# Decoder step on one core: attention by groups of 512 queries, the output projection between the groups, and part of a multiply on GpSimd

## The chip, the core and the metric

The kernel runs on one core of a Trainium2 chip. A core has five engines with in-order queues of their own: TensorE (PE in the profile; PEld are its weight loads), VectorE (DVE), ScalarE (ACT), GpSimd (POOL) and SyncE (SP), which here only issues DMAs. Engines wait for each other by semaphores. SBUF is the memory that all of them use, PSUM the one that TensorE writes; PSUM has eight banks of 128 x 512 float32. The metric is the device time of one execution, in microseconds, lower is better.

## What is computed

One step of a small decoder trunk: a state-space layer, a K/V projection and one layer of stick-breaking attention, for a prompt of 2048 tokens and eight single-token samples. The change lies in the attention layer of the prompt and the output projection behind it:

```python
def sb_attend(q, k, v, bias, q_pos, k_pos):       # 16 heads of 64
    z = einsum('bqhd,bkhd->bhqk', q, k) * HEAD_DIM ** -0.5 + bias
    mask = k_pos[None, :] < q_pos[:, None]        # strictly causal
    log_1m = where(mask, log_sigmoid(-z), 0.0)
    log_stick = cumsum(log_1m, axis=3, reverse=True) - log_1m
    w = where(mask, exp(log_sigmoid(z) + log_stick), 0.0)
    return einsum('bhqk,bkhd->bqhd', w, v)
...
x = x + gate * rms_norm((o * silu(z)) @ w_out_b, g_post_b)   # the projection, 1024 x 1024
```

The kernel forms s = sigmoid(z), c = 1 - s, a running product of c from the right (the stick that is left), and w = s times that product.

## The kernel before, in words

The last phase, `phase_b2`, holds the attention and the output projection. Its work is cut into 320 units. A unit is one head `h` of a head pair `hp`, one block `m` of 256 queries (or its upper or lower 128, `par`), and the lower or upper 1024 keys (`half`), of which `n` columns are not masked. Wide units (`par` is 0 or 1) have n = 640, 768, 896 or 1024; in narrow ones (`par` is None) both 128-row parts lie in one tile, with n = 256 or 512 each. The order of the units was: all of one head pair, block by block m = 0 to 7, upper keys before lower ones.

For each unit `front` does the following. TensorE forms the scores in PSUM tiles psZ (two float32r matmuls for each 512 columns, since the query is held as a high and a low part). ScalarE writes s = sigmoid of them. GpSimd writes c = 1 - s into a tile `cc` (L1417, and L1399 for narrow units); a memset puts 1.0 behind the last column (L1419, L1398). VectorE scans `cc` from the right with a product (L1426, L1402; its second operand `zero` lies in PSUM), and multiplies s by the scanned `cc` (L1427, L1403). Where a row of keys goes on in the other half, a copy of one column carries the product over (L1423).

```python
rev = cc[:, 0:n][:, ::-1]
nc.vector.tensor_tensor_scan(rev, rev, zero.to_broadcast([128, n]), init, OP.mult, OP.add)
nc.vector.tensor_mul(s[:, :n], s[:, :n], cc[:, 1:n + 1])
```

Three units later (`LAG`), `back` transposes the weights on TensorE (L54) and ScalarE copies them out of PSUM (L1443). Once both heads of a pair are there, `vals` multiplies them with the values. At the lower keys VectorE multiplies by the gate `zb` (L1469), the result is split in a high and a low part (L1470, L1471) and stored to `yT` in DRAM. Between units TensorE also works on the eight samples (`sample_vals`, pages of 2048 cached keys each) and the output weights are loaded and split (`stage_w`, L864 and L865).

Only when the attention is done come the 16 tiles of 128 rows of the output projection and one of 8 sample rows: `out_rows` loads a tile of `yT` and of the residual `x`, `out_proj` does 48 matmuls of 128 x 512, a norm (L906 to L912) and the sum with the residual, half on GpSimd and half on VectorE (L913).

Within one engine the instructions stand in the order that the scheduler of the framework gave them when the program was built; it is not the order of the Python text in every place. Each engine then works through its list in order.

Of the kernel before, what the change touches and what calls it, by code (L numbers as in the profile page):

```python
# [8 lines left out]
FT = mybir.dt.float32  # L9
# [8 lines left out]
D = 1024  # L18
SEQ = 2048
# [16 lines left out]
LAG = 3  # L36

# [5 lines left out]
class Kern:  # L43
# [29 lines left out]
    def run(self):  # L73
        with ExitStack() as ctx:
            tc = self.tc
            self.turn = 1
# [52 lines left out]
    def psZ(self):  # L129
        return self.ps.tile([128, 512], FT, tag="Z", name="psZ", bufs=3)  # L130
# [761 lines left out]
    def out_proj(self, xpool, M, yhi, ylo, cols, whi, wlo, x, G, dst, two=False):  # L892
# [3 lines left out]
        self.turn ^= 1  # L896
        if not two:
            p = self.psB()
            p = [p[:, 0], p[:, 1]]
        else:  # L900
            p = [self.psZ(), self.psZ()] if self.turn else [self.psA(), self.psA()]
        self.tm_r(p, M, yhi, ylo, cols, whi, wlo)
        ss = xpool.tile([128, 2], FT, tag="ss", name="ss")[:M]
        for h in range(2):
            jk = (self.rp.tile([128, 512], BF, tag="wraw", name="jk") if two else xpool.tile([128, 512], BF, tag="jk", name="jk"))[:M]
            nc.scalar.activation(jk, p[h][:M], AF.Square, accum_out=ss[:, h:h + 1])  # L906
        nc.vector.tensor_add(ss[:, 0:1], ss[:, 0:1], ss[:, 1:2])
        rs = self.rsqrt(xpool, ss[:, 0:1], M, 1, "rs")
        for h in range(2):
            c = slice(h * 512, h * 512 + 512)  # L910
            xo = self.rp.tile([128, 512], FT, tag="wraw", name="xo")[:M] if two else xpool.tile([128, 512], FT, tag="xo", name="xo")[:M]
# [149 lines left out]
    def phase_b1(self):  # L1061
# [7 lines left out]
        with ExitStack() as c:  # L1069
# [96 lines left out]
            for s, (ps, t) in enumerate(steps):  # L1166
# [14 lines left out]
                if s == 15:  # L1181
                    self.load_x(0, 0)
                    self.load_q(0, 0)
# [154 lines left out]
    def rot(self, kind, shape, dt=FR):  # L1338

        first, n = {"X": (0, 6), "V": (6, 3), "Q": (9, 2), "s": (11, 4), "y": (15, 1), "o": (0, 9)}[kind]  # L1340
# [4 lines left out]
    def load_x(self, hp, half):  # L1345

        nc = self.nc
        for h in (2 * hp, 2 * hp + 1):
            t = self.rot("X", [128, 1024])
            nc.sync.dma_start(t.bitcast(FT), dram(self.kT, h * 128 * SEQ + half * 1024, [[SEQ, 128], [1, 1024]]))  # L1350
            self.X[h, half] = t
        t = self.rot("V", [128, 8, 128], FT)
        nc.sync.dma_start(t, dram(self.O["p_v"], half * 1024 * D + hp * 128, [[D, 128], [128 * D, 8], [1, 128]]))
# [10 lines left out]

    def phase_b2(self):
        nc, tc, I, O = self.nc, self.tc, self.I, self.O
        self.yT = self.scr("yT", [2, D, NC1])
        with ExitStack() as c:
# [4 lines left out]
            samples = self.sample_vals(sp)  # L1373
            wload = self.stage_w("w1", I["w_out_b"], D, 0)
            X, V, Q = self.X, self.V, self.Q

            def front(u):
# [5 lines left out]
                cc = ap.tile([128, 1028], FT, tag="cc", name="cc", bufs=LAG + 2)  # L1383
                bias = self.sbias[:, h:h + 1]
                if par is None:
                    for a in range(2):
                        q = slice(a * 128, a * 128 + 128)
                        L = n if a else n - 128
                        z = self.psZ()
# [191 lines left out]
```

## Time and profile before

| | us |
|---|---|
| median of 3 runs (3326.25 to 3329.0) | 3328.98 |
| the profiled execution | 3336.95 |
| its span, first to last instruction | 3335.2 |
| last phase in it: attention, 1986.6 to 3139.1 | 1152.5 |
| last phase in it: the rest of the projection, 3139.1 to the end | 196.1 |

The profiled execution is 8 us slower than the median of the runs and 1.75 us longer than its own span. The last phase begins at 1986.6 us with the memset of `zero` (L1476); the last multiply of the attention on VectorE ends at 3139.1 us. A busy time is the time in which an engine had an instruction in it; for TensorE the ends of matmuls are modelled, so that the distance between starts says more.

### The profile page before, as it was taken

Reading aid. Unit: us, or ns where it says so; the run is one execution under the profiler, and the core shown is the slowest. Engines: PE = TensorE matmul, PEld = TensorE weight load, DVE = VectorE, ACT = ScalarE, POOL = GpSimd, SP = SyncE. Lnnn points to the kernel's source line nnn. Section 1 sums busy time; section 2 is a strip of 40 time slices with the busy share of each in tenths; the row PEclk is TensorE's granted clock in tenths of the full one; section 3 lists DMA queues with packets and bytes.
Section 4 is the critical chain, followed back from the end, with each engine's and each line's share of the span. In section 5 each row is a group of like instructions: output and inputs, shape, how many; then the busy total and the mean of one; then the engine's idle time right before and its main releaser. Section 6 shows DMA issues by size and latency. Waiting matters only on the chain.

```text
span 3335.2 us, 56710 instructions
## 1 busy us (share of the span) xinstructions
PE 2980.9 (89%) x19352; PEld 2349.6 (70%) x19352; DVE 2402.6 (72%) x4220; ACT 1310.6 (39%) x2954; POOL 682.5 (20%) x856
## 2 busy tenths in 40 slices
PE   7899899999999899988699998888888888888898
PEld 4667667778888898987588875555555555555677
DVE  7699997354445456666656539999999999899734
ACT  4422221332224433334232326556555655655311
POOL 1234343000000000001010103333223322333211
PEclk7999999999999899999899999999999999999999
DMA  7433333664543566667666674545345454534353
GB/s 216 133 95 106 99 95 93 193 186 122 157 140 110 173 188 191 192 201 218 189 198 197 200 209 135 157 126 166 116 135 156 137 151 123 160 113 121 89 170 127
DMA packets 488099, 506.91 MB, mean 152 GB/s; under 512 B 57605, under 2 KB 377382, under 8 KB 487618
## 3 DMA queue, kind: packets, MB, share of 16 engines
q1 hardware_dynamic: 482962, 501.88, 51.3%
q8 instruction: 154, 2.52, 0.3%
q10 hardware_dynamic: 4560, 1.35, 0.2%
q14 instruction: 135, 1.11, 0.1%
q0 software_dynamic: 288, 0.06, 0.0%
HBM read 372.39 MB, written 130.75 MB: 151 GB/s over the span
## 4 chain that ended last, share of the span: by engine, by line
PE 34%; DVE 32%; DMA 12%; issue 9%; ACT 4%; SPq 3%; POOL 2%; DVEq 0%; ACTq 0%; POOLq 0%
PE psA L49 20%; DVE cc L1426 9%; PE psB L49 5%; PE psZ L49 5%; DMA kp<-in_cache_k 5%; DVE s L1427 4%; PE psC L54 3%; DVE cc L1402 2%; DVE kp L1249 2%; PE psC L49 1%; DVE s L1403 1%; DVE zs L1250 1%; DVE A L563 1%; ACT s L1416 1%; POOL cc L1417 1%
## 5 line engine op out<-in xcount | busy, mean ns | idle before, releaser
L1426 DVE TENSOR_TENSOR_SCAN cc<-cc,zero 128x1024 f32<-128x1024 f32 (+3 forms) x256 | 538.0, 2108 | 49.4 <-POOL cc L1417 41.4
L54 PE MATMUL psC<-idf,s 128*128 128x128 f32 x2176 | 319.8, 287 | 146.3 <-ACT wT L1443 72.3
L1417 POOL TENSOR_SCALAR cc<-s 128x1024 f32<-128x1024 f32 (+3 forms) x256 | 291.0, 1139 | 643.4 <-ACT s L1416 401.3
L54 PEld LDWEIGHTS psC<-idf,s 128*128 128x128 f32 x2176 | 249.6, 146 | 211.5 <-ACT wT L1443 111.7
L49 PE MATMUL psZ<-X,Q 128*128 128x512 f32 (+2 forms) x1280 | 370.8, 409 | 20.3 <-ACT s L1416 15.5
L1416 ACT ACTIVATE s<-psZ,sbias 128x512 f32<-128x512 f32 (+2 forms) x512 | 310.1, 663 | 197.0 <-PE psZ L49 180.5
L1443 ACT ACTIVATE wT<-psC 128x512 f32<-128x512 f32 (+3 forms) x640 | 314.0, 549 | 64.4 <-PE psC L54 63.4
L1427 DVE TENSOR_TENSOR s<-s,cc 128x1024 f32<-128x1024 f32 (+3 forms) x256 | 305.3, 1201 | 13.6 <-DVE cc L1426 0.5
L1249 DVE TENSOR_TENSOR kp<-kp,qb 128x512 f32<-128x512 f32 x256 | 180.2, 708 | 186.3 <-DMA kp<-in_cache_k 159.9
L49 PE MATMUL psA<-hi,w0h 128*128 128x256 f32 (+1 forms) x1024 | 304.4, 297 | 10.6 <-DVE z L1103 3.8
L49 PEld LDWEIGHTS psZ<-X,Q 128*128 128x128 f32 x1280 | 220.6, 198 | 119.2 <-issue 74.2
L49 PE MATMUL psA<-hi,w0l 128*128 128x256 f32 (+1 forms) x1024 | 294.8, 288 | 2.6 <-DVE w0l L865 2.6
L49 PE MATMUL psA<-lo,w0h 128*128 128x256 f32 (+1 forms) x1024 | 294.8, 288 | 0.2 <-DVE lo L843 0.2
L49 PE MATMUL psA<-wT,V 128*64 128x256 f32 (+1 forms) x2304 | 285.1, 384 | 9.7 <-DVE cc L1423 5.8
L49 PEld LDWEIGHTS psA<-wT,V 128*64 128x64 f32 x2304 | 166.8, 141 | 109.2 <-issue 27.0
L1051 POOL TENSOR_TENSOR lo<-h,hi 128x256 fp32r<-128x256 f32 x92 | 75.8, 833 | 787.7 <-ACT hi L1050 642.1
L49 PEld LDWEIGHTS psA<-hi,w0h 128*128 128x128 f32 x1024 | 201.4, 197 | 13.0 <-DVE z L1103 4.6
L49 PEld LDWEIGHTS psA<-hi,w0l 128*128 128x128 f32 x1024 | 200.4, 196 | 3.3 <-DVE w0l L865 3.3
L49 PEld LDWEIGHTS psA<-lo,w0h 128*128 128x128 f32 x1024 | 201.2, 196 | 0.8 <-POOL lo L1051 0.5
L1250 DVE TENSOR_REDUCE zs<-kp 128x8 f32<-128x512 f32 x256 | 173.9, 683 | 5.6
L913 POOL TENSOR_TENSOR x<-x,xo 128x512 f32<-128x512 f32 x32 | 42.0, 1314 | 590.0 <-DVE xo L912 590.0
L49 PE MATMUL psA<-ghi,w0h 128*128 128x256 f32 (+1 forms) x512 | 149.6, 292 | 1.4 <-ACT sg L966 1.4
(412 smaller groups left out, 6784.0 us busy)
## 6 DMA issues: line engine op xcount, KB each, us to landing
kp<-in_cache_k SPq DMA_DIRECT2D x256, 256.0 KB
vp<-in_cache_v SPq DMA_DIRECT2D x256, 256.0 KB
Q<-qT SPq DMA_DIRECT2D x128, 256.0 KB
x<-x SPq DMA_DIRECT2D x50, 512.0 KB
x<-in_x_prompt SPq DMA_DIRECT2D x32, 512.0 KB
qT<-kq SPq DMA_DIRECT2D x128, 128.0 KB
kT<-kq SPq DMA_DIRECT2D x128, 128.0 KB
X<-kT SPq DMA_DIRECT2D x32, 512.0 KB
```

The lines of the kernel that those rows point to most:

```text
L49: self.nc.tensor.matmul(out, lhsT, rhs, start=start, stop=stop, skip_group_check=True)
L54: self.nc.tensor.transpose(out, in_, self.idf[b:b + n, b:b + n])
L913: (nc.vector if h else nc.gpsimd).tensor_add(x[:, c], x[:, c], xo)
L1051: (nc.gpsimd if k % 2 or kept else nc.vector).tensor_sub(lo[:, k, :256], h, hi[:, k, :256].bitcast(FT))
L1249: nc.vector.tensor_mul(kp, kp, qb)
L1250: nc.vector.tensor_reduce(zs[:, pg, a * 8:a * 8 + 8], kp.rearrange("p (h d) -> p h d", h=8), axis=mybir.AxisListType.X, op=OP.add)
L1402: nc.vector.tensor_tensor_scan(rev, rev, zero.to_broadcast([128, n]), 1.0, OP.mult, OP.add)
L1416: nc.scalar.activation(s[:, b:b + w], z, AF.Sigmoid, scale=0.125, bias=bias)
L1417: nc.gpsimd.tensor_scalar(cc[:, :n], s[:, :n], -1.0, 1.0, OP.mult, OP.add)
L1426: nc.vector.tensor_tensor_scan(rev, rev, zero.to_broadcast([128, n]), init, OP.mult, OP.add)
L1427: nc.vector.tensor_mul(s[:, :n], s[:, :n], cc[:, 1:n + 1])
L1443: nc.scalar.activation(wT[h][:, b:b + nb, a * 128:a * 128 + 128], p[:, :nb * 128].rearrange("p (b q) -> p b q", b=nb), AF.Copy)
```

## The change

Blocks of 256 queries are taken in pairs, in five groups: (3, 2), (7, 6), (5, 4), (1), (0). A group runs over all head pairs before the next begins, so that its 512 (or 256) rows of `yT` are complete when it ends. From the third group on, steps of the output projection of finished groups (`out_tiles`, 15 steps for a tile) are put between the units; the two tiles of the last group come at the end. The samples and the output weights are done in the first two groups (192 units). Keys, values, queries and gates are loaded by a look-ahead (`loads`), since they are now needed again in each group.

`front` is split in `score` and `weigh`: the text calls `weigh` of a unit behind `score` of the next one. The scan covers n + 1 columns, its start value comes from a small tile `car`. In `weigh` VectorE multiplies only the first `own` columns and GpSimd the rest: 640 and 384 of 1024, 640 and 256 of 896, 512 and 256 of 768, 512 and 128 of 640, 384 and 128 in each part of a narrow unit of 512. `cc` has 3 buffers instead of 5, psZ 2 instead of 3; the two value blocks of a group share one PSUM bank (`psO`). In the projection both halves of the sum with the residual are on GpSimd.

```diff
+GROUPS = ((3, 2), (7, 6), (5, 4), (1,), (0,))
+OUT_STEPS = 15
...
-            def front(u):
+            def score(u):
...
-                cc = ap.tile([128, 1028], FT, tag="cc", name="cc", bufs=LAG + 2)
+                cc = ap.tile([128, 1028], FT, tag="cc", name="cc", bufs=3)
...
+                nc.gpsimd.memset(cc[:, n:n + 1], 1.0)
                 nc.gpsimd.tensor_scalar(cc[:, :n], s[:, :n], -1.0, 1.0, OP.mult, OP.add)
-                if diag:
-                    nc.gpsimd.memset(cc[:, n:n + 1], 1.0)
-                    init = 1.0
-                else:
-                    prev = carry[h, par]
-                    nc.vector.tensor_copy(cc[:, n:n + 1], prev)
-                    init = prev
-                rev = cc[:, 0:n][:, ::-1]
-                nc.vector.tensor_tensor_scan(rev, rev, zero.to_broadcast([128, n]), init, OP.mult, OP.add)
-                nc.vector.tensor_mul(s[:, :n], s[:, :n], cc[:, 1:n + 1])
-                carry[h, par] = cc[:, 0:1]
-                return s
+                return s, cc
...
+            def weigh(u, s, cc):
+
+                hp, m, half, h, par, n = u
+                own = n - n // 128 * 3 // 8 * 128
...
+                first = half or m < 4
+                rev = cc[:, 0:n + 1][:, ::-1]
+                nc.vector.tensor_tensor_scan(rev, rev, zero.to_broadcast([128, n + 1]),
+                                             1.0 if first else carry.pop((h, m, par)), OP.mult, OP.add)
+                if half:
+                    carry[h, m, par] = ap.tile([128, 1], FT, tag="car", name="car", bufs=12)
+                    nc.vector.tensor_copy(carry[h, m, par], cc[:, 0:1])
+                nc.vector.tensor_mul(s[:, :own], s[:, :own], cc[:, 1:own + 1])
+                if own < n:
+                    nc.gpsimd.tensor_mul(s[:, own:n], s[:, own:n], cc[:, own + 1:n + 1])
...
             for i, u in enumerate(us):
...
+                s, cc = score(u)
+                pend.append((u, s))
+                loads(i + 1)
+                if scored:
+                    weigh(*scored)
+                scored = u, s, cc
...
+                if gi < 2:
+                    if i * 64 // (sw - 8) < (i + 1) * 64 // (sw - 8):
+                        next(samples, None)
+                    if i % 8 == 5:
+                        next(wload, None)
...
+                else:
+                    if i == starts[gi] + 8:
+                        t = [2 * mm + a for mm in GROUPS[gi - 1] for a in range(2)]
+                        tiles.extend(t)
+                        steps += OUT_STEPS * len(t)
+                    cols = n * (2 if par is None else 1)
+                    k = -(-steps * cols // left)
+                    left -= cols
+                    for _ in range(min(k, steps)):
+                        next(outs, None)
+                        steps -= 1
                 if len(pend) > LAG:
                     back(*pend.pop(0))
...
-            for i in range(1, 16):
-                if i < 15:
-                    ins.append(self.out_rows(xp, i + 1))
-                if i == 8:
-                    self.out_samples(rows, xp)
-                self.out_tile(rows, xp, i, *ins.pop(0))
+            tiles.extend(2 * GROUPS[-1][0] + a for a in range(2))
+            tiles.append(None)
+            flush(outs)
...
+    def out_tiles(self, rows, xp, tiles):
...
+            y = [xp.tile([128, KT, M], FR, tag=f"o{a}{M}", name=f"o{a}{M}") for a in range(2)]
+            for a in range(2):
+                self.nc.sync.dma_start(y[a].bitcast(FT), dram(self.yT, a * D * NC1 + t * 128, [[NC1, 128], [128 * NC1, KT], [1, M]]))
...
+            yield
+            if late:
+                next(late)
+            yield
+            if late:
+                next(late, None)
+            yield
+            p = [self.psA(), self.psA()]
...
+                    if i % 4 == 0 and i < 48:
+                        yield
+            late = self.out_end(rows, t, M, p, x, G)
+            yield
...
+            nc.vector.scalar_tensor_tensor(xo, p[h][:M], rs, G[:M, c], OP.mult, OP.mult)
+            nc.gpsimd.tensor_add(x[:, c], x[:, c], xo)
```

The first place is GpSimd's list in the middle of the attention. In the program before it held, for each unit, the operation c = 1 - s (`cc` from `s`) and a memset, and nothing that needs the scan of that unit:

```order
L1417 TENSOR_SCALAR cc_28533<-s_28532 128x1024
L1417 TENSOR_SCALAR cc_28559<-s_28558 128x1024
L1419 MEMSET cc_28598 128x1
L1417 TENSOR_SCALAR cc_28598<-s_28597 128x640
L1419 MEMSET cc_28625 128x1
L1417 TENSOR_SCALAR cc_28625<-s_28624 128x768
```

So GpSimd could make the next unit's c while VectorE was still scanning. The same engine in the second group of the changed program, with five successive units (their s is 28748, 28773, 28868, 28897 and 28929), where L1462 is the new multiply of a unit's last 384 columns and needs that unit's scan:

```order
L1462 TENSOR_TENSOR s_28748<-s_28748,cc_28749 128x384
L1429 MEMSET cc_28898 128x1
L1462 TENSOR_TENSOR s_28773<-s_28773,cc_28774 128x384
L1429 MEMSET cc_28930 128x1
L1430 TENSOR_SCALAR cc_28869<-s_28868 128x1024
L1430 TENSOR_SCALAR cc_28898<-s_28897 128x1024
L1462 TENSOR_TENSOR s_28868<-s_28868,cc_28869 128x384
L1429 MEMSET cc_29028 128x1
L1430 TENSOR_SCALAR cc_28930<-s_28929 128x1024
L1462 TENSOR_TENSOR s_28897<-s_28897,cc_28898 128x384
```

The multiply of unit 28773 now stands ahead of the c of the unit after it, 28868; for unit 28868 it is the other way round, since the c of 28897 is made first. Counted over the whole list, the c of the next unit stands behind the multiply of a unit in 151 of 288 places and ahead of it in 137. The list of VectorE for the same units:

```order
L1455 SCALAR_TENSOR_TENSOR cc_28774<-cc_28774,car_28461,zero_24053 128x1025
L1460 TENSOR_TENSOR s_28773<-s_28773,cc_28774 128x640
L1455 SCALAR_TENSOR_TENSOR cc_28869<-cc_28869,car_28493,zero_24053 128x1025
L1460 TENSOR_TENSOR s_28868<-s_28868,cc_28869 128x640
L1455 SCALAR_TENSOR_TENSOR cc_28898<-cc_28898,car_28527,zero_24053 128x1025
```

L1455 is the scan and L1460 the multiply of the first 640 columns: scan and multiply follow each other unit by unit as before, with 1025 and 640 columns in place of 1024 and 1024.

The second place is TensorE's list in the third group, where `o` is a tile of `yT` and psA the projection's result:

```order
L53 MATMUL psZ<-X,Q 128x512 x4
L53 MATMUL psA<-w1h_24059,o_34464 128x512 x2
L53 MATMUL psA<-w1h_24061,o_34463 128x512 x2
L53 MATMUL psA<-w1l_24062,o_34463 128x512 x2
L53 MATMUL psA<-w1h_24061,o_34464 128x512 x2
L58 MATMUL psC<-idf,s 128x128 x7
```

Between the scores of one unit and the transposes of an earlier one now stand eight of a tile's 48 matmuls; before, all of them stood behind the attention.

## Rows read from the trace of the kernel before

**Rows 1.** First part of the page: busy time of the engines over the span.

```profile
PE 2980.9 (89%) x19352; PEld 2349.6 (70%) x19352; DVE 2402.6 (72%) x4220; ACT 1310.6 (39%) x2954; POOL 682.5 (20%) x856
```

**Rows 2.** The last phase in two stretches: busy time by engine, clock, DMA.

```profile
core 0: us, PE busy (x) PEld busy (x) DVE busy (x) ACT busy (x) POOL busy (x), PEclk, DMA share, GB/s
1986.60:3139.10 1152.50, 976.21 (x6527) 655.99 (x6526) 1066.54 (x988) 662.48 (x1350) 364.05 (x512) 0.95 0.47 135
3139.10:3335.20 196.10, 186.11 (x843) 147.41 (x842) 78.76 (x258) 25.06 (x75) 21.97 (x17) 0.99 0.46 147
```

**Rows 3.** VectorE's groups in the last phase: count, busy us, mean ns, idle before.

```profile
L1426 DVE TENSOR_TENSOR_SCAN cc<-cc,zero 128x1024 f32<-128x1024 f32 x160 | 371.5, 2327 | 41.4 <-POOL cc L1417 41.4
L1427 DVE TENSOR_TENSOR s<-s,cc 128x1024 f32<-128x1024 f32 x160 | 205.5, 1293 | 8.0
...
L1403 DVE TENSOR_TENSOR s<-s,cc 128x1024 f32<-128x1024 f32 x32 | 41.9, 1309 | 1.9
...
L1427 DVE TENSOR_TENSOR s<-s,cc 128x896 f32<-128x896 f32 x32 | 36.0, 1125 | 1.7
L1427 DVE TENSOR_TENSOR s<-s,cc 128x768 f32<-128x768 f32 x32 | 35.2, 1099 | 1.8 <-DVE cc L1426 0.5
L1471 DVE TENSOR_TENSOR y<-zb,y 128x256 fp32r<-128x256 f32 x64 | 30.0, 468 | 15.2 <-ACT y L1470 15.2
L1427 DVE TENSOR_TENSOR s<-s,cc 128x640 f32<-128x640 f32 x32 | 29.4, 919 | 2.1
L1403 DVE TENSOR_TENSOR s<-s,cc 128x512 f32<-128x512 f32 x32 | 26.5, 828 | 2.0
L1469 DVE TENSOR_TENSOR zb<-zb,psA 128x256 f32<-128x256 f32 x64 | 25.9, 404 | 2.2 <-PE psA L49 2.2
L913 DVE TENSOR_TENSOR x<-x,xo 128x512 f32<-128x512 f32 x16 | 20.5, 1280 | 0.5
```

**Rows 4.** Timeline of VectorE and GpSimd at two places: start, duration, engine, instruction.

```profile
2192.29 1.04 POOL L1417 TENSOR_SCALAR cc<-s 128x1024 f32<-128x1024 f32 x1 [1.31 <-ACT s L1416]
2192.43 1.97 DVE L1403 TENSOR_TENSOR s<-s,cc 128x1024 f32<-128x1024 f32 x1
...
3124.02 2.35 DVE L1426 TENSOR_TENSOR_SCAN cc<-cc,zero 128x1024 f32<-128x1024 f32 x1 [0.88 <-POOL cc L1417]
3126.47 1.23 DVE L1427 TENSOR_TENSOR s<-s,cc 128x1024 f32<-128x1024 f32 x1
3126.52 3.09 POOL L1417 TENSOR_SCALAR cc<-s 128x1024 f32<-128x1024 f32 x2 [2.54 <-DVE cc L1426]
3128.64 2.35 DVE L1426 TENSOR_TENSOR_SCAN cc<-cc,zero 128x1024 f32<-128x1024 f32 x1 [0.88 <-POOL cc L1417]
```

**Rows 5.** GpSimd's subtractions of two SBUF tiles earlier: minimum, median, maximum in ns.

```profile
L1051 POOL TENSOR_TENSOR lo<-h,hi x92: 722/737/1282, 1070.7 to 1910.2; 128x256 fp32r<-128x256 f32 x92
...
L638 POOL TENSOR_TENSOR wl<-wraw,wh x32: 1257/1340/1625, 28.1 to 589.9; 128x512 fp32r<-128x512 f32 x32
```

**Rows 6.** GpSimd's timeline at narrower units.

```profile
2862.39 0.73 POOL L1417 TENSOR_SCALAR cc<-s 128x640 f32<-128x640 f32 x1 [3.33 <-ACT s L1416]
2863.06 0.10 POOL L1419 MEMSET cc<- 128x1 f32 x1
2867.38 0.83 POOL L1417 TENSOR_SCALAR cc<-s 128x768 f32<-128x768 f32 x1 [4.22 <-ACT s L1416]
```

**Rows 7.** TensorE's timeline in the attention.

```profile
2913.84 1.04 PE L54 MATMUL psC<-idf,s 128*128 128x128 f32 x8
2914.64 1.17 PE L49 MATMUL psZ<-X,Q 128*128 128x512 f32 x4
2915.66 1.04 PE L54 MATMUL psC<-idf,s 128*128 128x128 f32 x8
...
2920.19 3.67 PE L49 MATMUL psA<-wT,V 128*64 128x256 f32 x32
2923.79 1.19 PE L49 MATMUL psZ<-X,Q 128*128 128x512 f32 x4
```

**Rows 8.** The chain that ended last: start, us, what.

```profile
2729.49 4.38 DMA yT<-y
...
3031.26 4.89 DMA o<-yT
...
3303.51 10.88 PE psA L49 x48
3314.39 10.67 PE psZ L49 x47
```

More of the change, by code (lines that the diff above doesn't have):

```diff
@@ L1363, in load_q, with plan_b2 @@
             self.Q[2 * hp + a, m] = (t[:, a], t[:, 2 + a])
+    def plan_b2(self):
+        us, jobs, qs, starts = [], [], {}, []
+        for g in GROUPS:
+            starts.append(len(us))
+            for hp in range(NH // 2):
+                for half in ((1, 0) if g[0] >= 4 else (0,)):
+                    i0 = len(us)
+                    for m in g:
+                        for h in (2 * hp, 2 * hp + 1):
+                            for par in ((None,) if half == m // 4 and m % 4 < 2 else range(2)):
+                                qs.setdefault((hp, m), [len(us), 0])[1] = len(us)
+                                us.append((hp, m, half, h, par, min((2 * m + (par is None or par) + 1) * 128 - half * 1024, 1024)))
+                    jobs.append((hp, half, max(u[5] for u in us[i0:]), i0, len(us) - 1))
+        return us, jobs, list(qs.items()), starts
     def phase_b2(self):
@@ L1367, in phase_b2 @@
         self.yT = self.scr("yT", [2, D, NC1])
+        X, V, Q = self.X, self.V, self.Q
+        us, jobs, qs, starts = self.plan_b2()
+        NU = len(us)
         with ExitStack() as c:
@@ new lines, in flush @@
+            def flush(*gens):
+                for g in gens:
+                    for _ in g:
+                        pass
+            zero = self.ps.tile([128, 512], FT, tag="zero", name="zero", bufs=1)[:, 0:1]
+            nc.vector.memset(zero, 0.0)
+            carry, wT, o_, late, zbs, rest = {}, {}, {}, [], {}, []
+            nx, nv, nq = [1], [1], [2]
+            samples = self.sample_vals(sp)
+            wload = self.stage_w("w1", I["w_out_b"], D, 0)
+            first = {v[0]: k for k, v in qs}
@@ L1495, in phase_b2 @@
-                pend.append((u, front(u)))
+                if i in starts:
+                    gi += 1
+                    if gi >= 2:
+                        left = sum(v[5] * (2 if v[4] is None else 1) for v, k in zip(us, range(NU))
+                                   if starts[gi] <= k < (starts + [NU])[gi + 1])
+                if i in first:
+                    t = zbs[first[i]] = rows.tile([128, 256], FT, tag="zb", name="zb", bufs=4)
+                    nc.sync.dma_start(t, self.zbT[hp * 128:hp * 128 + 128, m * 256:m * 256 + 256])
@@ L1510, in phase_b2 @@
[L1510 removed]
+            weigh(*scored)
             for x in pend:
```

218 lines of the change are left out of this document (121 added, 97 removed).

## Prediction

> **What bounds the kernel now.** I read the page's busy line first [rows 1]. Over the whole span TensorE has 89% and GpSimd 20%, but the change touches only the last phase, so I asked for that phase in two stretches [rows 2]. In the attention VectorE works 1066.5 of 1152.5 us and waits 86; TensorE works 976 by modelled ends, GpSimd 364. In the 196.1 us behind it TensorE works 186 and VectorE 79. So one stretch is VectorE's and the other TensorE's, and laying the second under the first could give up to 196 us, if VectorE's stretch grows no longer.
>
> Then VectorE's groups [rows 3]: a full unit costs a scan of 2.33 us and a multiply of 1.29, and of the idle time before scans 41.4 us end with GpSimd's c = 1 - s. Last, the timeline where such a wait stands [rows 4]. After a scan VectorE's multiply starts at 3126.47, and GpSimd's c, 0.05 later, is not done 1.04 us after its start: two of them take 3.09 together, and the next scan waits 0.88. At 2192.29 GpSimd came first: its 1.04 stayed, and VectorE's multiply took 1.97. So VectorE's multiply of two SBUF tiles and GpSimd's reading operation exclude each other, and the first holds to its end.
>
> The Trainium skill, "SBUF — State Buffer", section "Who interferes with whom", says the same: a VectorE instruction with two SBUF inputs contends with a GpSimd instruction that reads SBUF, and the one issued first blocks the other fully. These rows agree. By that rule a multiply split over the two engines would not run side by side at all; without it the GpSimd part would be hidden beside VectorE's, and the sum would come out as in the first rival below.
>
> **The change, part by part** (against the profiled 3336.95).
>
> *Tail removed:* -196.1 [rows 2].
>
> *Shorter multiplies on VectorE:* widths become those of rows that exist, 1024 to 640, 896 to 640, 768 and 640 to 512, narrow 1024 to 768. By the means of [rows 3]: 160 x (1.293 - 0.919) = 60; 32 x (1.125 - 0.919) = 7; 32 x (1.099 - 0.828) = 9; 32 x (0.919 - 0.828) = 3; 32 x (1.309 - 1.099) = 7. Sum -86. The narrow 512 keeps its width. The column copies for the carry are about as many as before, and one more scan column of 1024 is 2 ns (2327 / 1024): nothing for both.
>
> *The multiply on GpSimd, and what is queued behind it:* GpSimd's list is in order, and in 151 of 288 places the c of the next unit stands behind the multiply of this one. There the next scan waits for a chain: VectorE's multiply, then GpSimd's (it is excluded, or at best starts 0.05 later), then a memset in about half the places, then c. Durations: c of 1024 takes 1.04 [rows 4], of 640 0.73, the memset 0.10 [rows 6]; a two-input operation of 256 columns 0.74 and of 512 1.26 [rows 5], so 384 about 1.0 and 128 about 0.45, estimates by that line. The two c's behind a multiply end 1.91 after it [rows 4] (3126.52 + 3.09 less 3127.70), 0.17 under their sum of 2.08, so I take off 0.17. A multiply of 384: 1.0 + 0.1 + 1.04 - 0.17 = 1.95 of wait. In 86 places it is 384 wide (168 us), in 45 256 (1.6 each, 72) and in 20 128 (1.15 each, 23): 263. In 52 of the places other VectorE work stands in between (37 splits of y at 0.47, 34 gates at 0.40 [rows 3], 13 sums of the projection, 112 small ones at about 0.1 by estimate): it fills about 45. About half of the 41.4 us of waits for c [rows 3] fell in such places and were there already: -20. Left +198. The bounds: if both multiplies ran side by side, GpSimd's would end 1.15 after the scan, memset and c at 2.29, against VectorE's end at about 0.95: 1.34 a place instead of 1.95. From above, GpSimd might also come first in the other 137 places (second rival).
>
> *Projection under the attention:* VectorE keeps (78.76 - 20.5) / 17 = 3.4 us a tile, since the sums with the residual [rows 3] go to GpSimd: 15 tiles, +51. GpSimd gets 2 x 1.29 a tile, off the path at 364 of 1152 us.
>
> *TensorE:* a full wide unit is a score of 1.02, transposes of 0.80 and a quarter of two heads' value matmuls, 3.60 / 4 = 0.90 [rows 7]: 2.72 against VectorE's 3.3 (2.33 + 0.92) and its waits. In the third group four tiles and the sample rows, 5 x 10.88 [rows 8] over 80 units, add 0.7: still under VectorE's. No cost there. But all steps of the last two groups fall behind their eighth unit, that is into 8 units each: in the fourth group 8 x 2.7 + 4 x 10.9 = 65, and since `y` has one buffer for each part, about 12 of its loads of 4.89 [rows 8] open, 77 against some 52 of VectorE's; in the fifth 41 against 28. Together +36 to +40; I take 36.
>
> *The new tail:* from the last multiply to the store of yT 2, the store 4.4, the load 4.9, a tile 10.9, the next load 4.9 (one buffer), a tile 10.9, and from the end of the last matmuls to the end of the span 10.1 (3335.2 less 3325.06) [rows 8]: +48.
>
> *Loads:* X, V and Q come again in each group, so more is moved than 135 GB/s at a share of 0.47 [rows 2]; they start 16 to 24 units ahead, over 50 us, against 4.89 for a load. Nothing; if that cover goes it is one load of about 5 us for each of 64 jobs at worst, part of the third rival.
>
> *Sum:* -196 - 86 + 198 + 51 + 36 + 48 = +51: 3388 as profiled. The profile stands 8 us above the median, so the median becomes 3329 + 51 = **3380**.
>
> The break-even: gains net of the tail are 196 - 135 = 61, with 86 and 20 more 167; against it stand 151 w - 45. It is even at w = 1.4 us a place; my mean is 263 / 151 = 1.74.
>
> **The rivals.** (1) *No full exclusion for the GpSimd multiply*, so faster: a wait of 1.34 instead of 1.95 in the 86 places (-52), about 0.55 less in 45 (-25) and 0.5 in 20 (-10), and the 20 us of old exclusion waits gone as well: 3380 - 107 = 3273, about 3270. For it: no row shows a two-input operation of GpSimd beside VectorE's multiply. Against: [rows 4] show both orders of the exclusion for its one-input operation. Chance 0.20. It decides from w below 1.4.
>
> (2) *GpSimd takes the memory first in the other places*, so slower still: there its c may be under way as the scan ends, as at 2192.29, and the multiply waits; or the multiply is delayed behind c and the following c with it. 74 x 1.0 + 51 x 0.7 + 12 x 0.4 = 115 more, 3495. Against: after a scan VectorE starts at 0.10 and GpSimd at 0.15 [rows 4]. Chance 0.12.
>
> (3) *TensorE or loads become the bound in the third group*, since a step waits for a `y` load between a unit's scores and its transposes: 8 tiles' pairs of loads at 4.9, and as much again from X and V, +40: 3420. Against: every load is asked for one tile or 16 units ahead. Chance 0.06.
>
> My forecast has 0.62, with a range of its own of 3316 to 3435 (w from 1.38 to 2.04, which is 54 below and 45 above, and tail and blocks 10 either way).
>
> **How the numbers follow.** About 0.2%, 7 us, is what a measurement of this kernel can tell from no change. Faster: all of rival (1) but its upper edge, 0.19, and the low edge of my case, 0.10: 0.29. Same (3322 to 3336): 0.07. Slower: 0.64. The range goes from 3260, which holds most of rival (1), to 3465, which leaves out rival (2) and the tails of the others.
>
> **What the changed profile would show.** VectorE's idle time before the scans L1455 and L1443, released by GpSimd's `cc` L1430, grows from 41 us to some 200, in stretches of 1.5 to 2 us, in the first three groups. VectorE's 640-column multiply is at 0.85 to 0.92. GpSimd's multiply L1462, started 0.05 behind VectorE's, lasts some 1.8 us: blocked, then 1.0. TensorE's busy share in the first two groups falls. The last two groups show blocks of 48 matmuls, and 45 to 50 us lie behind the last multiply. Wrong I would be if the idle time before scans stays under 150 us, if L1462 lasts 1.0 beside a multiply that also runs, or if waits on TensorE stand before the scans.

## The result and the profile after

The changed kernel takes 3514.25 us (3511.22 to 3520.91), against 3328.99 us before: a ratio of 1.0561, 95% interval 1.0543 to 1.0579. It is slower, as forecast, but by 185 us where 51 were forecast, and it lies above the whole range of 3260 to 3465.

The busy line of the page after answers to [rows 1]:

```profile
PE 3191.4 (91%) x19352; PEld 2374.1 (68%) x19352; DVE 2320.4 (66%) x4203; ACT 1331.3 (38%) x2954; POOL 1034.8 (29%) x1289
```

TensorE has as many matmuls as before and 210 us more busy time. That is the first thing that the prediction did not have. The last phase in windows answers to [rows 2]: the first two groups together (1989.31 to 2824.77), the third, the fourth and fifth, and what lies behind the last multiply (the columns are the window, its length, then PE, PEld, DVE, ACT and POOL with busy time and count, the granted clock, the DMA share and GB/s):

```profile
1989.31:2824.77 835.46, 798.29 (x4141) 413.62 (x4140) 588.59 (x544) 415.40 (x810) 431.05 (x577) 0.98 0.56 163
2824.77:3286.84 462.07, 391.39 (x2272) 282.10 (x2271) 344.92 (x445) 222.84 (x441) 235.35 (x291) 0.91 0.37 108
3286.84:3453.26 166.42, 147.74 (x808) 106.80 (x807) 110.75 (x193) 60.93 (x150) 59.59 (x85) 0.94 0.72 193
3453.26:3511.30 58.04, 32.16 (x129) 23.57 (x127) 11.82 (x46) 6.04 (x20) 7.65 (x6) 0.82 0.26 82
```

In the first two groups TensorE works 798 of 835 us and VectorE only 589: the bound has changed its engine. Where TensorE's time comes from is seen in its timeline. Here are the first two of the four calls of a step of the sample pages (`vp,W`: each on 32 columns of the array, shown as x2 for one call) in the changed kernel:

```profile
2060.74 0.82 PE L53 MATMUL psO<-wT,V 128*64 128x256 f32 x6
2061.49 1.04 PE L53 MATMUL psA<-vp,W 128*32 128x512 f32 x2
2062.46 0.65 PE L53 MATMUL psO<-wT,V 128*64 128x256 f32 x4
2063.04 1.04 PE L53 MATMUL psA<-vp,W 128*32 128x512 f32 x2
2064.01 0.43 PE L53 MATMUL psO<-wT,V 128*64 128x128 f32 x2
2064.38 1.08 PE L53 MATMUL psZ<-X,Q 128*128 128x512 f32 x4
```

and a step in the kernel before, its four calls in one row (x8):

```profile
2063.91 1.06 PE L49 MATMUL psA<-vp,W 128*32 128x512 f32 x8
2064.90 0.85 PE L49 MATMUL psZ<-X,Q 128*128 128x384 f32 x4
```

From start to the next start one call alone takes 0.97 us (2061.49 to 2062.46), and all four in a row 0.99 (2063.91 to 2064.90): four calls on four parts of the array run side by side if they stand next to each other. Before, 52 of the 64 steps stood so, and twelve as one call and three; now 224 calls stand alone between other matmuls. Over all steps, from start to next start, the calls hold TensorE for 241 us instead of 83. The Trainium skill, "TensorEngine Tiling (Array Packing)", section "Key Properties", says that tiles work in parallel and that a change of the tiling mode drains the engine. The rows agree with the first; what a change of mode costs by itself no row shows. The prediction did not look at these calls in TensorE's list at all.

VectorE's scans answer to [rows 3]:

```profile
L1455 DVE TENSOR_TENSOR_SCAN cc<-cc,car,zero 128x1025 f32<-128x1025 f32 x128 | 299.8, 2345 | 134.0 <-POOL cc L1430 102.8 <-POOL cc L1429 26.0 <-POOL cc L1416 5.3
L1460 DVE TENSOR_TENSOR s<-s,cc 128x640 f32<-128x640 f32 x192 | 175.9, 920 | 12.2
L1443 DVE TENSOR_TENSOR_SCAN cc<-cc,zero 128x512 f32<-128x512 f32 x64 | 74.7, 1207 | 30.0 <-POOL cc L1417 20.3 <-POOL cc L1416 9.6
...
L1455 DVE TENSOR_TENSOR_SCAN cc<-cc,zero 128x897 f32<-128x897 f32 x32 | 64.5, 2016 | 30.9 <-POOL cc L1430 27.2 <-POOL cc L1429 3.6
```

Over all its forms the scan now waits 282 us for GpSimd, against 54 before. Counted place by place in the trace, 255 of them stand before the 151 scans whose c is queued behind a multiply, 1.69 each, and 6 before the 137 scans whose c was made first. The place that the prediction described is there, in VectorE's and GpSimd's timeline:

```profile
2716.92 0.82 DVE L1460 TENSOR_TENSOR s<-s,cc 128x640 f32<-128x640 f32 x1
2716.97 1.51 POOL L1462 TENSOR_TENSOR s<-s,cc 128x384 f32<-128x384 f32 x1 [2.53 <-DVE cc L1455]
2718.45 1.03 POOL L1430 TENSOR_SCALAR cc<-s 128x1024 f32<-128x1024 f32 x1
2719.44 0.09 POOL L1429 MEMSET cc<- 128x1 f32 x1
2719.52 2.35 DVE L1455 TENSOR_TENSOR_SCAN cc<-cc,car,zero 128x1025 f32<-128x1025 f32 x1 [1.77 <-POOL cc L1429]
```

VectorE's multiply starts first and GpSimd's 0.05 later; it lasts 1.51 instead of 0.86 (the row "2336.25 0.86" of this trace, where VectorE scans and does not multiply), so that it ends 0.74 behind VectorE's; full exclusion would make that 0.86. Then comes c, and the scan has waited 1.77, where the prediction had 1.95. What the Trainium skill, "SBUF — State Buffer", section "Who interferes with whom", says of two engines that read SBUF this way holds here to within 0.12 us: the one that issued first had it to its end.

The end of the chain that ended last:

```profile
3462.27 0.97 DVE y L1510
3463.26 2.23 DMA yT<-y
3465.62 4.45 DMA o<-yT
3470.20 12.86 PE psA L53 x47
...
3487.59 12.85 PE psA L53 x47
```

The last two tiles take 12.9 each, not the 10.88 of [rows 8]; the granted clock of this window is 0.82, in [rows 2] it was 0.99. Three stretches, ahead of the last tile and in it (columns as above), show where the difference lies:

```profile
3483.00:3487.60 4.60, 0.29 (x3) 0.01 (x1) 2.72 (x14) 1.27 (x4) 0.00 (x0) 0.99 0.80 213
3487.60:3491.00 3.40, 3.40 (x8) 2.48 (x9) 0.59 (x1) 0.00 (x0) 2.51 (x2) 0.51 0.10 27
3491.00:3494.00 3.00, 3.00 (x15) 2.44 (x14) 0.00 (x0) 0.00 (x0) 0.00 (x0) 1.00 0.43 173
```

TensorE works 0.29 of 4.6 us while the tile is loaded; then it makes 8 matmuls in 3.4 us at 0.51 (the level of 1.2 GHz), and 15 in the next 3.0 us at 1.00 (2.4 GHz). Between the last multiply (3453.26) and the store of y (3463.26) lie 10 us, where the prediction put 2: there stand nine matmuls of a tile, the last values and, in VectorE's list, the norm of a tile and its `xo` (L1665) ahead of the last y.

### The profile page after: what moved, and what is told of

It is laid out like the page before. It is cut to its first block, busy times and chain, and to the rows that moved or that the text cites. A ratio compares the mean times of both kernels' runs of the same rounds, so it can differ in the third digit from the quotient of the medians.

```text
span 3511.3 us, 57543 instructions
## 1 busy us (share of the span) xinstructions
PE 3191.4 (91%) x19352; PEld 2374.1 (68%) x19352; DVE 2320.4 (66%) x4203; ACT 1331.3 (38%) x2954; POOL 1034.8 (29%) x1289
## 4 chain that ended last, share of the span: by engine, by line
PE 45%; DVE 25%; DMA 11%; issue 6%; POOL 4%; ACT 3%; SPq 3%; POOLq 0%; ACTq 0%; DVEq 0%
PE psA L53 23%; PE psZ L53 6%; DVE cc L1455 5%; PE psC L58 5%; PE psO L53 5%; PE psB L53 5%; DMA kp<-in_cache_k 4%; DVE kp L1250 2%; DVE s L1460 1%; POOL cc L1430 1%; DVE cc L1443 1%; PE psC L53 1%; DVE zs L1251 1%; DVE A L566 1%; POOL s L1462 1%
## 5 line engine op out<-in xcount | busy, mean ns | idle before, releaser
L53 PE MATMUL psZ<-X,Q 128*128 128x512 f32 (+2 forms) x1280 | 385.7, 411 | 39.7 <-ACT s L1414 33.6
L1462 POOL TENSOR_TENSOR s<-s,cc 128x384 f32<-128x384 f32 (+2 forms) x256 | 319.0, 1246 | 330.3 <-DVE cc L1455 260.9
L1455 DVE TENSOR_TENSOR_SCAN cc<-cc,car,zero 128x1025 f32<-128x1025 f32 x128 | 299.8, 2345 | 134.0 <-POOL cc L1430 102.8
L1430 POOL TENSOR_SCALAR cc<-s 128x1024 f32<-128x1024 f32 (+3 forms) x256 | 257.5, 1007 | 237.7 <-ACT s L1428 235.6
L53 PE MATMUL psO<-wT,V 128*64 128x256 f32 (+1 forms) x2304 | 320.9, 385 | 2.1 <-ACT wT L1476 1.9
L1455 DVE TENSOR_TENSOR_SCAN cc<-cc,zero 128x897 f32<-128x897 f32 (+3 forms) x128 | 240.7, 1884 | 93.2 <-POOL cc L1430 59.4
L53 PEld LDWEIGHTS psO<-wT,V 128*64 128x64 f32 x2304 | 166.3, 140 | 146.6 <-issue 81.0
L53 PE MATMUL psA<-vp,W 128*32 128x512 f32 x512 | 244.4, 604 | 0.2 <-DMA vp<-in_cache_v 0.2
L1460 DVE TENSOR_TENSOR s<-s,cc 128x640 f32<-128x640 f32 (+1 forms) x256 | 221.0, 867 | 14.4
L53 PE MATMUL psA<-w1h,o 128*128 128x512 f32 (+1 forms) x544 | 171.4, 425 | 36.3 <-DVE xo L1665 24.1
```

Of the source, the lines that this page charges most:

```text
L53: self.nc.tensor.matmul(out, lhsT, rhs, start=start, stop=stop, skip_group_check=True)
L1430: nc.gpsimd.tensor_scalar(cc[:, :n], s[:, :n], -1.0, 1.0, OP.mult, OP.add)
L1460: nc.vector.tensor_mul(s[:, :own], s[:, :own], cc[:, 1:own + 1])
L1462: nc.gpsimd.tensor_mul(s[:, own:n], s[:, own:n], cc[:, own + 1:n + 1])
```

## The experiments

Theory A, formed from this profile: TensorE bounds the first two groups, because the sample pages, pressed into 192 of 320 units, hold it three times as long. Theory B is the prediction's: the place of c behind the multiply on GpSimd. Differences in us across runs are differences of the ratios to the kernel before, times 3333 us.

| kernel | median us | ratio to before | 95% interval |
|---|---|---|---|
| changed | 3514.25 | 1.0561 | 1.0543 to 1.0579 |
| e1 pages together | 3471.38 | 1.0417 | 1.0395 to 1.0439 |
| e2 no multiply on GpSimd | 3471.22 | 1.0409 | 1.0374 to 1.0444 |
| e3 both | 3396.54 | 1.0191 | 1.0171 to 1.0211 |
| e4 pages together, c first | 3354.02 | 1.0058 | 1.0038 to 1.0079 |
| e5 before, with the divided multiply, c first | 3284.98 | 0.9855 | 0.9839 to 0.9872 |
| e6 before, page calls apart | 3331.27 | 0.9990 | 0.9980 to 0.9999 |
| e7 before, two psZ | 3336.61 | 1.0006 | 0.9992 to 1.0020 |
| e8 e4 with 1 of 16 pages | 3266.53 | 0.9793 | 0.9777 to 0.9809 |
| e9 e4, all page loads, 1 of 16 calls | 3349.47 | 1.0049 | 1.0031 to 1.0067 |
| e10 e4, all page calls, 1 of 16 loads | 3274.93 | 0.9839 | 0.9808 to 0.9870 |
| e11 changed, c first | 3445.77 | 1.0338 | 1.0315 to 1.0361 |
| e12 e4, projection at the end | 3476.07 | 1.0432 | 1.0407 to 1.0456 |
| e13 e4, scores first | 3304.83 | 0.9906 | 0.9889 to 0.9922 |
| e14 e4, X, Q, V on ScalarE's queue | 3391.48 | 1.0170 | 1.0153 to 1.0187 |
| e15 changed, scores first | 3487.65 | 1.0460 | 1.0443 to 1.0478 |

**Pages together (e1).** `behind` is an edge that sets the order of instructions in a list and adds no wait:

```diff
-                    for s in range(4):
-                        self.mm(p[s * 32:s * 32 + 32], W[:, s, pg * 16:pg * 16 + 32], vps[s], pg == 0, pg == NPG - 1)
+                    calls = []
+                    for s in (3, 2, 1, 0):
+                        calls.append(nc.tensor.matmul(p[s * 32:s * 32 + 32], W[:, s, pg * 16:pg * 16 + 32], vps[s],
+                                                      start=pg == 0, stop=pg == NPG - 1, skip_group_check=True))
+                        if s < 3:
+                            self.tc.add_manual_dep(calls[-1].ins, calls[0].ins.name, behind, reason="last page first")
```

> The changed kernel, but the four sample-page calls of a step stand next to each other on TensorE again, as before the change (the call of the last page first, the others may not be put ahead of it). Theory A (TensorE: split page calls; one alone takes 0.98 us, four in a row 1.0 us, so 241 us instead of 83, all in the first two groups, which TensorE bounds): TensorE's page work falls to 83 us, groups 1 and 2 from 835 us to 700 to 730 (then VectorE's 589 us of work and its waits for c), the time to 3390 to 3420. Theory B (the queue on GpSimd that the prediction named is the whole loss): groups 1 and 2 hardly move, 3490 to 3515.

Measured: 48 us less, 3471, between what the two theories gave. The window of the first two groups:

```profile
1983.09:2777.76 794.67, 654.18 (x4148) 419.52 (x4149) 586.12 (x544) 409.80 (x812) 430.05 (x579) 0.91 0.59 172
```

TensorE's work fell by 144 us as expected, the groups by only 41. TensorE no longer bounds them, and VectorE with 586 of 795 us doesn't either: waits between the engines do. A explains a part, and under it lies something else.

**No multiply on GpSimd (e2), and both (e3).**

```diff
-                own = n - n // 128 * 3 // 8 * 128
+                own = n
```

> The changed kernel with the whole multiply on VectorE again (own = n), page calls left split. Theory A: groups 1 and 2 stay bound by TensorE at 800 to 835 us; only the third group gains, its waits for c (98 us) less 25 us of longer multiplies: 3430 to 3480. Theory B: all waits of VectorE for c but some 40 us go (275 to 40) and 86 us of multiply come back: 3514 - 150 = 3365.

> Pages together and no multiply on GpSimd. If A and B are both at work: VectorE's busy time 1044 + 86 = 1130 us, some 60 us of waits, 36 us for the blocks of projection in the last groups and 58 us of tail: 1285 us for the last phase instead of 1349 before, 3265 (3240 to 3300). A alone would put it beside the run with pages together and the GpSimd multiply; B alone beside the run without that multiply.

Measured: e2 saves 51 us, within A's range and far from B's 3365; e3 saves 123. The windows of groups 1 and 2 of e2, then of e3:

```profile
1988.47:2823.91 835.44, 799.57 (x4150) 411.00 (x4148) 642.30 (x544) 414.30 (x811) 212.16 (x386) 0.99 0.56 163
```

```profile
1987.44:2746.06 758.62, 651.76 (x4148) 417.76 (x4148) 630.98 (x544) 407.91 (x812) 202.38 (x387) 0.93 0.62 180
```

In e2 these groups take 835.4 us, to a tenth what they took with GpSimd's multiply: while TensorE bounds them, what GpSimd does costs little there (e11 below gains 10 us in them). All of e2's gain lies behind them. With the pages together the multiply costs 75 us (e1 to e3). So A and B are both at work, and each hides a part of the other. But e3 is far above the 3265 expected.

**c first (e4).** The multiply of a unit may not be put ahead of the c of the next:

```diff
-                nc.gpsimd.tensor_scalar(cc[:, :n], s[:, :n], -1.0, 1.0, OP.mult, OP.add)
+                made[0] = nc.gpsimd.tensor_scalar(cc[:, :n], s[:, :n], -1.0, 1.0, OP.mult, OP.add)
...
+            def after_c(x, cc):
+                self.tc.add_manual_dep(x.ins, made[0].ins.name, behind, reason="next c first")
...
-                    nc.gpsimd.tensor_mul(s[:, own:n], s[:, own:n], cc[:, own + 1:n + 1])
+                    after_c(nc.gpsimd.tensor_mul(s[:, own:n], s[:, own:n], cc[:, own + 1:n + 1]), cc)
```

> Pages together, GpSimd multiplies its columns as in the changed kernel, but its list always has the c of the next unit ahead of this unit's multiply (288 of 288 places). Theory B (order in the list): the waits before the scans fall below 80 us though GpSimd does the same work, VectorE has 1044 us of work, TensorE some 1210: 3200 to 3270, below the run without the multiply. Rival, by the exclusion alone (rival 2 of the prediction): the multiply and c collide in the new places too, waits stay at 150 us or more, 3330 or above.

Measured: 120 us below e1, whose edit it has with one for GpSimd's list, and 44 below e3, but far above the 3200 to 3270 expected. The waits before scans fall from 260 us (e1) to 154, not below 80. The multiply on GpSimd is thus a gain of 44 us in the right order and a loss of 75 in the one that was built. By the bounds set ahead (150 us, 3330) the rival would hold; the traces say otherwise. In the changed kernel only 6 us of waits stand at the 137 places where c comes first, and VectorE's multiplies are together 31 us longer than the shortest of their width, against 36 in the kernel before and 33 in e4. e5 below, with c first everywhere, has 85 us of waits. So collisions are not what is left in e4; e8 to e13 look for it.

**The parts by themselves in the kernel before (e5, e6, e7).** e5 has `score` and `weigh` of the change for `front`, with c first as in e4, and none of the groups:

```diff
-                pend.append((u, front(u)))
+                s, cc = score(u)
+                pend.append((u, s))
+                if scored:
+                    weigh(*scored)
+                scored = u, s, cc
```

e6 puts the four page calls at four turns of the generator:

```diff
                     for s in range(4):
                         self.mm(p[s * 32:s * 32 + 32], W[:, s, pg * 16:pg * 16 + 32], vps[s], pg == 0, pg == NPG - 1)
-                    yield
+                        yield
...
-                if (i + 1) * 13 // 60 > i * 13 // 60:
+                if (i + 1) * 52 // 60 > i * 52 // 60:
```

e7 is one number, `bufs=3` to `bufs=2` for psZ.

> The kernel before, with nothing of the groups: only scan and multiply of a unit are written behind the scores of the next, the multiply is divided as in the change, and on GpSimd c of the next unit always stands ahead of the multiply. If a multiply on GpSimd pays once its place in the list is right: VectorE has 86 us less to do (1067 to 980 in the attention), its waits before scans stay below 80 us, 3245 to 3285. If the two engines' exclusion eats it: 3320 to 3345.

> The kernel before, in which only the four page calls of a step are put in four different places (one for each turn of the generator, four times as many turns). Theory A (a page call alone holds TensorE 0.98 us): TensorE has 976 + 150 us of work under 1152 us of attention, and the time rises by 40 to 90 us, 3370 to 3420. If what a call costs alone is hidden under VectorE: 3325 to 3340.

> The kernel before with two score tiles in PSUM (psZ) in place of three, as the change has it: it gave the third bank to psO. If that is part of the loss: TensorE's waits for the sigmoid grow from 16 us, the waits of VectorE for c with them, 3345 to 3390. If VectorE covers it: 3325 to 3340.

Measured: e5 0.9855, 48 us faster than before and the fastest kernel here that computes all; it keeps the order of units and takes of the change only `score` and `weigh` with the divided multiply. Its time is at the upper edge of what was expected, its waits before scans, 85 us, just above the 80. The windows of the attention in e5 and in e6 (compare [rows 2]):

```profile
1988.13:3087.44 1099.31, 966.40 (x6512) 652.14 (x6502) 969.95 (x984) 653.88 (x1343) 676.34 (x922) 0.95 0.49 141
```

```profile
1987.69:3131.32 1143.63, 1110.43 (x6525) 658.39 (x6525) 1056.05 (x983) 664.52 (x1345) 370.23 (x506) 1.00 0.47 136
```

In e5 VectorE's work falls from 1067 to 970, 97 us, and 53 of them reach the attention's length. In e6 TensorE works 134 us more and the time doesn't change: over 320 units there is room for it. A's price is paid only where the pages are pressed into 192 units; the 40 to 90 us expected for e6 by theory A were wrong. psZ with two buffers costs nothing (e7).

**What is left in groups 1 and 2 of e4: 736 us against 583 of VectorE's work (e8, e9, e10).** e8 leaves out 15 of 16 pages of each sample, loads and calls; e9 only their calls; e10 only their loads (the calls read the first page again). In e8, e9 and e10 the sample rows of y are therefore made from the first page alone.

```diff
-                for pg in range(NPG):
+                for pg in range(1):
```

```diff
+                    if pg:
+                        yield
+                        continue
                     calls = []
```

```diff
-                    vps = []
-                    for s in range(4):
+                    vps = [] if pg == 0 else vps
+                    for s in range(4 if pg == 0 else 0):
```

> The kernel with pages together and c first, with 1 of 16 cache pages of each sample (the other 15 are left out: no loads and no calls for them). If the samples, pressed into 192 of 320 units, are what keeps its first two groups at 736 us against 583 us of VectorE's work: they fall below 670, the time to 3290 or less. If it is the order of units and buffers: they stay above 700, 3320 or more.

> The kernel with pages together and c first; all cache pages are loaded, but the calls on TensorE for 15 of 16 pages of each sample are left out. Groups 1 and 2 took 736 us with all of it and 647 us without loads and calls. If the loads (the queue, the memory) make the difference: above 700 us here, 3320 or more. If the calls on TensorE do: below 670, 3290 or less.

> The same kernel with all calls but loads for 1 of 16 pages only (the calls read the first page again). If TensorE's 70 us of calls make the difference: groups 1 and 2 above 700 us, 3320 or more. If the loads do: below 670 us, 3290 or less.

The windows of groups 1 and 2 of e4, e8, e9 and e10, in this order:

```profile
1994.21:2729.76 735.55, 637.98 (x4147) 406.64 (x4147) 582.90 (x544) 405.13 (x812) 407.14 (x579) 0.94 0.64 185
```

```profile
1993.70:2640.49 646.79, 568.50 (x3667) 404.75 (x3666) 582.48 (x546) 407.38 (x814) 418.15 (x576) 0.93 0.42 115
```

```profile
1986.65:2714.86 728.21, 602.28 (x3693) 405.83 (x3693) 583.67 (x544) 411.05 (x809) 406.05 (x577) 0.93 0.64 186
```

```profile
1990.39:2646.96 656.57, 598.07 (x4143) 398.54 (x4142) 578.67 (x544) 403.63 (x812) 415.12 (x577) 0.96 0.41 112
```

It is the loads, not the calls: with them 728 to 736, without 647 to 657. That is 73 us in the time (e4 to e10), and the prediction had put "Nothing" for loads. The kernel before has the same page loads over 320 units, and no run leaves them out there.

**The two causes one by one in the changed kernel (e11), and the projection (e12).** e11 is e4 without the pages' edit. e12 takes the steps of the projection out from between the units, so that all tiles come at the end, with two tiles of yT in flight:

```diff
-                    for _ in range(min(k, steps)):
-                        next(outs, None)
-                        steps -= 1
...
-            y = [xp.tile([128, KT, M], FR, tag=f"o{a}{M}", name=f"o{a}{M}") for a in range(2)]
+            y = [self.rot("o", [128, KT, 128])[:, :, :M] for a in range(2)]
```

> The changed kernel with only GpSimd's list put right (c of the next unit ahead of the multiply); the page calls stay split. If groups 1 and 2 are bound by TensorE (798 us of work): they stay above 790 us and the third group falls from 462 to some 410, 3410 to 3440 in all. If the order on GpSimd was the larger cost there too: groups 1 and 2 at 750 or less, 3400 or less.

> The kernel with pages together and c first, but no step of the projection between the units: all tiles come at the end as before the change (two tiles of yT in flight). Groups 3 to 5 took 569 us with it in between, and 58 us lay behind. If laying it under the attention pays: 16 x 10.9 us come back at the end and the units give less than that, 3390 or more. If it only slows the units as much as it saves: 3340 to 3370. If it costs more than it saves: 3330 or less.

e11 saves 74 us. Its first two groups still take 825, bound by TensorE; the gain is in the third group, 462 to 408 us. In e12 the third group, the fourth and fifth, and the end take

```profile
2720.24:3050.61 330.37, 294.13 (x1823) 198.88 (x1822) 294.26 (x319) 203.67 (x400) 213.27 (x272) 0.95 0.37 102
3050.61:3172.57 121.96, 97.83 (x573) 61.49 (x573) 91.99 (x125) 60.63 (x139) 46.91 (x73) 0.86 0.69 170
3172.57:3469.60 297.03, 216.26 (x804) 164.04 (x801) 56.98 (x240) 22.36 (x70) 42.70 (x34) 0.88 0.36 112
```

and in e4, with the projection in between,

```profile
2729.76:3138.15 408.39, 374.13 (x2265) 272.87 (x2265) 343.91 (x445) 219.98 (x440) 227.54 (x291) 0.96 0.43 122
3138.15:3298.62 160.47, 143.73 (x807) 104.43 (x806) 109.40 (x193) 60.59 (x149) 56.36 (x83) 0.97 0.74 199
3298.62:3356.70 58.08, 31.52 (x128) 23.05 (x126) 11.80 (x46) 6.04 (x20) 7.66 (x6) 0.82 0.26 82
```

By e12's expectation (3390 or more) laying the projection under the attention pays. The third group holds nine tiles' steps (432 matmuls of the projection in e4's trace: the sample rows, four tiles of group 1 and four of group 2), the last two groups six. The steps add 78 and 39 us to the units, 117 in all. e12's own end is no measure, since its 297 us have only one pair of psA where the kernel before took psZ and psA in turn (TensorE waits 70 us in it for VectorE to free psA). Against the 196.1 of [rows 2] the end shrinks by 138: of the 196 us laid under the attention 138 - 117 = 21 are a gain.

**Late loads or a late place in the list (e13, e14, e15).** In TensorE's list of e4 the scores of 33 of the 192 units of the first two groups stand one to three units later than in the rest, behind transposes that wait for VectorE (39 in the changed kernel); in e8 and e10, without the loads, three do, and in the kernel before four of 320. e13 sets that right and leaves the loads as they are:

```diff
                 s, cc = score(u)
+                newest[0] = self.last
...
-                            self.tr(p[:, i * 128:i * 128 + 128], s[:, so + (b + i) * 128:so + (b + i) * 128 + 128])
+                            x = self.tr(p[:, i * 128:i * 128 + 128], s[:, so + (b + i) * 128:so + (b + i) * 128 + 128])
+                            self.tc.add_manual_dep(x.ins, newest[0].ins.name, behind, reason='scores first')
```

e14 loads X, Q and V by ScalarE's queue, here X:

```diff
-            self.nc.sync.dma_start(t[:, :width].bitcast(FT),
+            self.nc.scalar.dma_start(t[:, :width].bitcast(FT),
```

e15 is the changed kernel with e13's edit alone.

> The kernel with pages together and c first, and in TensorE's list the transposes of a unit always behind the scores of the third unit after it; all loads as they were. If only the order in the list was the loss: groups 1 and 2 fall from 736 us to 640 to 670, 3265 to 3295 in all. If the tiles really land late: TensorE waits for X or Q instead, groups 1 and 2 at 710 or more, 3330 or more.

> The kernel with pages together and c first, with X, Q and V loaded by ScalarE's queue, so that they never stand behind a page load or a store of yT on SP; by this the list of TensorE has the scores in time as well, without being forced. If the order was the loss: 3265 to 3300, like the run with scores first. If SP's queue held them up on the chip: clearly below that run, by 20 us or more. If the memory is too slow for all loads: 3330 or more.

> The changed kernel with the scores forced ahead in TensorE's list only; page calls stay split, c stays behind the multiply in half of the places. TensorE has some 798 us of work in groups 1 and 2, so they can fall from 835 to no less than about 800: 3480 to 3515. If the late scores were the main loss by themselves: 3430 or less.

Groups 1 and 2 of e13:

```profile
1997.93:2686.68 688.75, 615.05 (x4146) 402.10 (x4145) 583.58 (x544) 400.52 (x811) 411.36 (x577) 0.96 0.68 198
```

They take 689 us, between both expectations; the time falls by 51 us, to 0.9906. The order accounts for most of what the loads did; without the loads (e10) it would be 22 us less still, and for those the runs don't tell the queue from the memory. e14 is 37 us slower than e4. Among its waits in groups 1 and 2 is

```profile
PE psA L1324 <- DMA vp<-in_cache_v: 61.0, 18, 5.9
```

(engine, waited for, us, times, longest), where e4 has

```profile
PE psA L1324 <- DMA vp<-in_cache_v: 7.2, 3, 3.1
```

So with X, Q and V on a second queue the pages come later, and TensorE waits for them. Whether they are late because the loads share the memory, or because the list asks for them sooner, these runs don't say. Nor do they part this from a third: issuing the loads takes 67 us in ScalarE's list in these groups, and ScalarE also writes s. e15 saves 34 us in the changed kernel.

## Why the prediction was wrong

The queue on GpSimd works as the prediction said, but its sum failed at three steps, two of which it put at nothing. That the sign came out right is in part luck: with the queue put right (e11) the kernel is still 3.4% slower, by what the prediction did not have, and the forecast without its queue term would have been faster.

- **"TensorE ... No cost there."** That step counted the matmuls of a unit and of the projection, and left the sample pages out. Their calls, four side by side before, stand apart in the changed list and cost 241 us instead of 83, in groups that TensorE then bounds with 798 of 835 us. Its busy share there rose to 96%, from 85% over the attention before, where the prediction said that it falls. Setting it right gives 48 us in the changed kernel and 93 once c stands first (e11 to e4). No rival named it; the third spoke of TensorE in the third group only. For that group the step counted five tiles, and nine are there: 98 us by its own 10.88, not 54. TensorE then works 374 us in it (e4) and VectorE 344, so that "still under VectorE's" fails there too.
- **"Loads: ... Nothing."** That step looked at X, V and Q, not at the page loads that now stand among them in 192 units. Without page loads e4 is 73 us faster (e10), and 51 of these come back with all loads when the scores stand in time in TensorE's list (e13). Of the 22 us left no run shows what part the change added. The prediction read GpSimd's and VectorE's lists, and TensorE's only in the third group.
- **Projection under the attention.** The forecast had fifteen tiles at 3.4 of VectorE, nine of which fall in the third group: 31 us there, and 20 + 36 in the last two, 87 in all. The runs show 78 and 39: 117. In the third group TensorE works 374 of 408 us, so a tile costs about what TensorE needs for it. The tail was 58 us instead of 48: 10 us from the last multiply to the store where 2 were put, and 12.9 a tile, less 2 for a shorter store.
- **The multiplies** were right: -86 forecast, -97 in e5 (all of VectorE's work in the attention).
- **The queue on GpSimd** was right in its mechanism and, as waits, near in size: 1.69 a place over 151 places, 255 us, where the forecast had 1.74 and 263, less 45 that other work fills. But a wait that is taken away is not all gained: the term was 198, and the order gives 120 from e1 to e4 and 74 in the changed kernel (e11), since other waits come in its place and in the first two groups TensorE's work covers it. Against no multiply on GpSimd it is some 140 (75 from e1 to e3, and the 65 us that VectorE works less in e1). The term was too large by some 60 to 120, and that hid a part of what was missing.

Together: e13, with pages, c and scores in order, stands at 0.9906, about 3298 us; the forecast without its queue term would be 3182. Of these 116 us, 30 are the projection's and 10 the tail's. In groups 1 and 2 e13 leaves VectorE idle for 105 us, where a forecast without the queue keeps 86 x 583 / 980 = 51: 54 more. The last 22 are not assigned.

Of the rivals, the first (no full exclusion) is refuted by the multiply of 1.51 beside 0.86. Its ground was that no row shows a two-input operation of GpSimd beside VectorE's multiply, but the trace of the kernel before has one beside VectorE's sum:

```profile
3329.62 1.26 POOL L913 TENSOR_TENSOR x<-x,xo 128x512 f32<-128x512 f32 x1 [9.58 <-DVE xo L912]
3330.18 1.25 DVE L913 TENSOR_TENSOR x<-x,xo 128x512 f32<-128x512 f32 x1
```

VectorE's sum of 512 columns takes 1.25 there, where a multiply of that width takes 0.83 on average [rows 3], and ends 0.55 behind GpSimd's. The second is refuted by the 6 us at the 137 places where c comes first. The third had the right group and, with 40 us, nearly the size (78 us where the forecast had 31), but not the cause: in e4 TensorE's projection matmuls wait there for VectorE's `xo`, and not for a load of `y`.

## What to carry to other kernels

When work is pressed into fewer stages, count every call of every engine in those stages, and read how the calls stand in each list: calls that run side by side only when they are neighbours can be torn apart by nothing but a change of pace. An operation given to an idle engine with an in-order queue pays or costs by what stands behind it: the same multiply was worth -44 us or +75. And an end that one engine holds alone is not free to hide: here 117 of 138 us came back.

## What the hardware showed unexpectedly

- One float32 call of 128 x 512 on 32 columns of the array takes 0.97 us between other calls, and four on four parts 0.99.
- The exclusion of VectorE's two-input multiply and GpSimd's multiply is as strict as for a one-input operation: 0.86 without a multiply beside it, 1.51 when started 0.05 behind one, of which 0.74 lie behind VectorE's end.
- 134 us more of TensorE's work in the attention (e6) cost nothing, at 1110 of 1144 us busy: the engines' waits overlapped that well.
